# Reordering the first attention of a diffusion backbone, moving conditioning-vector work to the norms, and placing tiles at multiples of 256 bytes

## The chip, the cores and the metric

The kernel runs on one core of one Trainium2 chip, in one launch. Five engines matter: TensorE does matmuls and transposes (PE, with its weight loads as PEld), VectorE is DVE, ScalarE is ACT, GpSimd is POOL, and SyncE (SP) issues nearly all DMAs. Each engine takes its instructions in the order of the program, so an instruction that waits holds up all that stand behind it on its engine. The metric is device microseconds of one execution, lower is better.

## The reference, cut to what matters

256 latent tokens and 256 context tokens, width 1024, two layers. A vector per token kind, SiLU(c) or SiLU(c_ctx), is multiplied by `ada_w` (1024 x 6144 per layer) and gives six conditioning vectors `m[0..5]`: shift, scale and gate ahead of and behind each sub-layer.

```
for l in 0, 1:
    m = split(silu(c) @ ada_w[l] + ada_b[l], 6)         # for latent and for context tokens
    h = rms_norm(x, norm1_g[l]) * (1 + m[1]) + m[0]
    y = even_mixer(h) if l == 0 else odd_mixer(h)       # conv + grouped-query attention; differential attention
    x = x + m[2] * y
    h = rms_norm(x, norm2_g[l]) * (1 + m[4]) + m[3]
    x = x + m[5] * (swiglu(h) if l == 0 else moe(h))    # hidden width 3584; 8 experts, top 2
out = rms_norm(x_latent, final_norm_g)
```

The first attention has 8 query heads of 64 over 2 key heads. Latent queries see 512 keys, context queries 256. Each query and key head is RMS-normed, and latent ones are rotated.

## The kernel before, in words

All is float32. A matrix product is made of three fp32r matmuls (`mm3`, L222 to L225): a value is split into a rounded high part and the rest (`parts`, L233: an ACT copy, then a DVE subtraction). Weights come as blocks of 1 MB. `Stream` holds five landing buffers (`raw0` to `raw4`) and some tiles lent for one load each (`spare`, `once`); `pump` issues the next load on SP as soon as a landing buffer is free, in the order in which the program first uses the blocks. `ws.step()` does the pending DVE part of a split (`low`, L152) and starts the next split (ACT, L140); `ws.get()` forces it.

The order of all engines is the order in which the Python code emits (a manual schedule). The stages, with their places in the profiled span: first norm, convolution and projections up to about 160 us; the first attention (160 to 249); its output projection (to 298); the norm of the dense SwiGLU and the SwiGLU (`ffn_chunk`, 15 steps, to 820); the norm ahead of the second attention and that attention (to about 1030); its output projection, the norm of the experts and the router (to 1061); the experts (to the end).

Conditioning vectors. `ada_half` (L329) makes half of one vector in four yields: 16 matmuls of 512 columns that read two `raw` blocks as they are (L339), an ACT copy (L343), four transposes, two small DVE operations. Such halves wait in `fillers`; `fill(n)` runs the next n of these parts wherever it is called. Before the change, `fill` is called in the first attention from iteration 6 on (six halves), in the output projection, in the SwiGLU (six halves), and in the second attention (four).

First attention. `attend(i)` is one iteration of a pipeline over 32 units (a block of 128 queries and a head; context units are 16 to 31). A unit passes `ev_A` (scores, PE, two units at once into two "mm" banks), `ev_max` (DVE), `ev_exp` (ACT), `ev_C` (transposes, PE, into one of two "tr" banks), `ev_parts` (ACT and DVE, reads that bank), `ev_D` (times values, PE, "av" bank), each one iteration later than the one before; `ev_E` finishes four heads. The order inside an iteration is exp, C, A, E, max, parts, D. PSUM has 8 banks: four "mm", two "tr", one "av", one "ad". The query projections sit in `bq = [PS("av"), PS("ad"), PS("mm"), PS("mm")]`, so the last two share the banks that scores use; `q_b(3)` reads the last of them in iteration 2.

Norms. `rms_rows` takes a square with a row sum (ACT, L400), a power (POOL, L390) and a scaling (DVE, L404) for each block of 128 tokens. `norm_into` then transposes, evacuates and splits, and feeds the first matmuls of the stage behind it. Between a stage's last matmul and the first transposes stands `residual` (L947, L948) of the last block and this chain.

Of the kernel before, what the change touches and what calls it, by code (L numbers as in the profile page):

```python
# [195 lines left out]
def build(nc, tc, a, out, order, dbg=None, stop=None):  # L196
# [18 lines left out]
    def SM(n, name="sm", dt=F32):  # L215
        return pool.tile([128, n], dt, name=name, tag=f"sm{n}_{dt}", bufs=12)
# [3 lines left out]
    mm = nc.tensor.matmul  # L220
# [31 lines left out]

    raws = [T([128, 2048], f"raw{i}") for i in range(5)]
# [9 lines left out]
    cst = T([128, 272], "cst")  # L263
# [45 lines left out]
    mhalf = T([128, 16], "mhalf")  # L309
# [10 lines left out]
    lnT = T([128, 8], "lnT")  # L320
# [39 lines left out]
    def run(g, n=10 ** 9):  # L360
        for _ in range(n):
            try:
                next(g)
            except StopIteration:
                return False
        return True

# [173 lines left out]
    ypad = T([128, 4, 2, 286], "ypad", tag="cA")  # L541
# [4 lines left out]
    cw = T([128, 4, 31], "cw")  # L546
# [3 lines left out]
    nc.vector.tensor_copy(cw, p.rearrange("p (j w) -> p j w", j=4)[:, :, 0:31])  # L550
# [4 lines left out]
    diag = T([128, 32], "diag")  # L555
# [139 lines left out]
    def q_proj(t):  # L695
        for k in range(8):
            mm3(bq[t], [x[:, k, t * 128:(t + 1) * 128] for x in hT], [x[:, k % 2, :] for x in un[k // 2]],
                k == 0, k == 7)
# [58 lines left out]
    bq = [PS("av"), PS("ad"), PS("mm"), PS("mm")]  # L757
# [137 lines left out]
    def attend(i):  # L895
        if 2 <= i < n + 2:
            ev_exp(i - 2)
        if 3 <= i < n + 3:
            ev_C(i - 3)
        if i < n and i % 2 == 0:  # L900
            ev_A(i)
        if "E" in last:
            run(last["E"], 1)
        if 1 <= i < n + 1:
            ev_max(i - 1)
        if 4 <= i < n + 4:
            ev_parts(i - 4)
        if 5 <= i < n + 5:
            ev_D(i - 5)
            if i % 4 == 0:  # L910
                last["E"] = ev_E((i - 5) // 8, (i - 5) // 4 % 2)
        if i in (2, 4):
            last["T"] = q_T(2 + i // 4)
        if i in (3, 5):
            last["T"]()
        if i == 2:
            q_b(3)
        ws.step()
        if 8 <= i < 16 and i % 2:
            j = (i - 8) // 2  # L920
            parts(cat[0][:, j, :], cat[1][:, j, :], cs[:, j])
        if i >= 6:
            fill(1)

    for k in range(8):
        mm3(bq[3], [x[:, k, 384:512] for x in hT], [x[:, k % 2, :] for x in un[k // 2]], k == 0, k == 7)
        if k % 2:
            ws.done(("win", 2, k // 4), k // 2 % 2)
        if 2 <= k <= 5:
            ln_cols(k - 2)  # L930
        if k == 5:
            attend(0)
# [24 lines left out]
    fillers += [ada_half(0, 5, 0)]  # L957
# [13 lines left out]
    for i, kk in enumerate((0, 1, 2, 3)):  # L971
        un = w_out_w(0, kk)
        for t in range(4):
            w_out(0, kk, t, bo[t], un, i == 0, i == 3)
        ws.done(("wout", 0, 0, kk // 2), kk % 2)
        ws.step()
        if i >= 1:
            run(gg, 2)
        fill(2)
    for t in range(4):  # L980
        residual(t, 0, 512, bo[t], g)
    fill(10 ** 6)
    uns = {kk: w_out_w(1, kk) for kk in (0, 1, 2, 3)}
    fillers += [ada_half(0, 5, 1)]
    for t in range(4):
        bank = PS("mm")
        for i, kk in enumerate((0, 1, 2, 3)):
            w_out(1, kk, t, bank, uns[kk], i == 0, i == 3)
            if t == 3:
                ws.done(("wout", 0, 1, kk // 2), kk % 2)  # L990
                ws.step()
        residual(t, 512, 1024, bank, g, nc.vector)
        run(rr, 1)
    run(rr)
# [9 lines left out]
    fill(10 ** 6)  # L1004
    h2 = new_h("h2")
    first = [PS("mm") for _ in range(2)]
    un0 = [[t.rearrange("p (k n) -> p k n", k=4) for t in ws.get(("fg", 0), h)] for h in range(2)]
# [8 lines left out]
    fillers += [ada(1, m) for m in (1, 0, 2)]  # L1016
# [4 lines left out]
    def ffn_chunk(c):  # L1021
# [29 lines left out]
        if c >= 1:  # L1051
            hl = hid.pop(c - 1)
            un = [ws.get(("fd", c - 1), h) for h in range(2)]
            i = 0
            for t in range(4):
                for o in range(2):
                    p = PS(("tr", "tr", "av")[i % 3])
                    for f in range(2):
                        mm3(p, [x[:, f, t * 128:(t + 1) * 128] for x in hl],
                            [x[:, o * 512:(o + 1) * 512] for x in un[f]], f == 0, f == 1)  # L1060
                    residual(t, o * 512, o * 512 + 512, p, g, nc.vector if c == 14 else None)
                    i += 1
                    if i in (2, 4):
                        ws.step()
                    if i == 6 or i == 3 and c % 3 == 0:
                        fill(1)
                if c == 14:
                    run(rr, 1)
            ws.done(("fd", c - 1), 0, 1)
            ws.step(2)  # L1070
# [8 lines left out]
    fill(10 ** 6)  # L1079
    for t in range(4):  # L1080
        dump(f"x2_{t}", X[t])
# [7 lines left out]
    fillers += [ada(1, m) for m in (4, 3)]  # L1089
    fill(2)  # L1090
# [256 lines left out]

    while plan:
# [31 lines left out]
    w_done(1, 3)  # L1380
    for t in range(2):
        residual(t, 512, 1024, bo[1, t], g, nc.vector)
        run(rr, 1)
    for t in range(2):
        dump(f"x3_{t}", X[t])
# [11 lines left out]
    run(a15[0], 1)  # L1397
# [8 lines left out]
    run(a15[1], 1)  # L1406
# [502 lines left out]
```

## Time and profile before

| | us |
|---|---|
| median of 3 runs | 2080.54 |
| lowest and highest run | 2078.64, 2083.23 |
| the profiled execution's own time | 2079.71 |
| its span from first to last instruction | 2077.9 |

The span is the profiled execution; its own time is 1.8 us longer, for what lies around it. PE is busy 96% of the span, DVE 71%, ACT 55%, POOL 12%. A busy PE is not always a PE at full speed: the profile also gives the clock that TensorE was granted in a stretch (1.00 is 2.4 GHz, 0.50 is 1.2 GHz).

### The profile page before, as it was taken

To read this page: it belongs to the slowest core of one execution; us is meant where nothing else is said; L and a number is where in the kernel's file an instruction comes from. 1 tells how busy PE (TensorE), PEld (TensorE's weight loads), DVE (VectorE), ACT (ScalarE), POOL (GpSimd) and SP (SyncE) were. 2 spreads that over 40 slices of the span, in tenths; PEclk is the share of its full clock that TensorE was granted. 3 is DMA by queue.
4 is the path that set the end of the run, shared out by engine and by line. 5 is a ranking of instruction groups with operands and counts; after the bars stand their busy time and mean duration, and the time that the engine had idled before them with its cause. 6 is when DMAs were issued, how large, how long until landed. Compare 5 with 4: busy or idle time off the path is not lost.

```text
span 2077.9 us, 28499 instructions
## 1 busy us (share of the span) xinstructions
PE 1995.2 (96%) x10806; PEld 1606.3 (77%) x10806; DVE 1476.7 (71%) x1918; ACT 1147.5 (55%) x1576; POOL 245.1 (12%) x222
## 2 busy tenths in 40 slices
PE   6998899999999998999989999999999999999987
PEld 4866677777777776989868888888888888888876
DVE  3535443545545456666568999998989999999997
ACT  3215433222222223434457878778787878878765
POOL 0310010323324243011110000000000000000020
PEclk9999899999999999999889999999999999999999
DMA  8303632334333223332488999999999999999972
GB/s 313 124 21 122 231 135 84 139 121 141 132 113 101 81 102 116 119 139 98 143 328 293 353 361 346 358 364 365 356 350 353 372 362 352 346 358 370 351 302 90
DMA packets 98639, 483.39 MB, mean 233 GB/s; under 512 B 12170, under 2 KB 12834, under 8 KB 51649
## 3 DMA queue, kind: packets, MB, share of 16 engines
q1 hardware_dynamic: 96128, 479.84, 63.0%
q8 instruction: 86, 1.41, 0.3%
q10 hardware_dynamic: 2368, 1.68, 0.3%
q14 instruction: 57, 0.46, 0.1%
HBM read 480.43 MB, written 1.05 MB: 232 GB/s over the span
## 4 chain that ended last, share of the span: by engine, by line
PE 57%; DVE 2%; ACT 1%; issue 0%; DVEq 0%; POOL 0%; ACTq 0%; POOLq 0%
PE mm L223 12%; PE mm L224 12%; PE mm L225 12%; PE av L225 3%; PE av L224 3%; PE av L223 3%; PE ad L223 2%; PE ad L224 2%; PE ad L225 2%; PE tr L313 2%; DVE wlo L152 1%; PE tr L1592 1%; PE tr L1518 1%; PE tr L1470 0%; PE ad L339 0%
## 5 line engine op out<-in xcount | busy, mean ns | idle before, releaser
L140 ACT CAST whi<-raw 128x1024 fp32r<-128x1024 f32 x420 | 434.8, 1049 | 248.7 <-PE tr L225 102.8
L152 DVE TENSOR_TENSOR wlo<-raw,whi 128x1024 fp32r<-128x1024 f32 x420 | 550.7, 1346 | 11.9 <-ACT whi L140 8.4
L224 PE MATMUL mm<-wlo,xghi 128*128 128x512 f32 x896 | 351.8, 393 | 5.1 <-DVE wlo L152 5.0
L223 PE MATMUL mm<-whi,xghi 128*128 128x512 f32 x896 | 355.4, 397 | 0.0
L225 PE MATMUL mm<-whi,xglo 128*128 128x512 f32 x896 | 351.0, 392 | 0.0
L948 POOL TENSOR_TENSOR x<-x,tmp 128x512 f32<-128x512 f32 x110 | 163.4, 1516 | 468.1 <-DVE tmp L947 467.8
L140 ACT CAST whi<-spare 128x512 fp32r<-128x512 f32 (+1 forms) x282 | 188.9, 708 | 46.8 <-PE mm L225 27.7
L152 DVE TENSOR_TENSOR wlo<-spare,whi 128x512 fp32r<-128x512 f32 (+1 forms) x282 | 212.5, 794 | 0.0
L224 PEld LDWEIGHTS mm<-wlo,xghi 128*128 128x128 f32 x896 | 168.9, 189 | 43.2 <-DVE wlo L152 8.2
L225 PEld LDWEIGHTS mm<-whi,xglo 128*128 128x128 f32 x896 | 168.8, 188 | 37.1
L223 PEld LDWEIGHTS mm<-whi,xghi 128*128 128x128 f32 x896 | 168.9, 189 | 35.4
L223 PE MATMUL mm<-h2hi,whi 128*128 128x512 f32 x448 | 179.4, 401 | 0.9 <-ACT h2hi L234 0.9
L224 PE MATMUL mm<-h2lo,whi 128*128 128x512 f32 x448 | 178.2, 398 | 0.3 <-DVE h2lo L235 0.2
L225 PE MATMUL mm<-h2hi,wlo 128*128 128x512 f32 x448 | 177.6, 396 | 0.0
L1044 DVE TENSOR_TENSOR silu<-mm,silu 128x512 f32<-128x512 f32 x28 | 19.4, 692 | 191.5 <-PE mm L225 191.5
L152 DVE TENSOR_TENSOR wlo<-rawx,whi 128x1024 fp32r<-128x1024 f32 x112 | 135.1, 1221 | 5.0 <-ACT whi L140 1.6
L140 ACT CAST whi<-rawx 128x1024 fp32r<-128x1024 f32 x112 | 117.4, 1052 | 31.9 <-PE mm L225 27.6
L1605 POOL MEMSET fgain<- 128x1 f32 x1 | 0.1, 98 | 906.9 <-DVE wlo L152 906.9
L223 PEld LDWEIGHTS mm<-h2hi,whi 128*128 128x128 f32 x448 | 84.7, 189 | 24.2 <-issue 3.4
L224 PEld LDWEIGHTS mm<-h2lo,whi 128*128 128x128 f32 x448 | 84.7, 189 | 20.8 <-DVE h2lo L235 1.1
L225 PEld LDWEIGHTS mm<-h2hi,wlo 128*128 128x128 f32 x448 | 84.7, 189 | 20.2
L223 PE MATMUL mm<-whi,h3hi 128*128 128x256 f32 x320 | 93.7, 293 | 1.3 <-ACT h3hi L234 1.3
(395 smaller groups left out, 3849.4 us busy)
## 6 DMA issues: line engine op xcount, KB each, us to landing
raw<-in_t_g_dram SPq DMA_DIRECT2D x81, 1024.0 KB, 7.4
rawx<-in_t_u_dram SPq DMA_DIRECT2D x53, 1024.0 KB, 6.9
raw<-in_t_ada_dram SPq DMA_DIRECT2D x38, 1024.0 KB, 4.9
raw<-in_t_u_dram SPq DMA_DIRECT2D x30, 1024.0 KB, 7.5
raw<-in_t_d_dram SPq DMA_DIRECT2D x30, 1024.0 KB, 7.2
spare<-in_t_g_dram SPq DMA_DIRECT2D x56, 512.0 KB, 7.0
spare<-in_t_u_dram SPq DMA_DIRECT2D x112, 256.0 KB, 6.8
rawb<-in_t_d_dram SPq DMA_DIRECT2D x27, 1024.0 KB, 7.2
```

The lines of the kernel that those rows point to most:

```text
L140: self.nc.scalar.copy(hi[:, i * n:(i + 1) * n], x)
L152: self.nc.vector.tensor_tensor(lo[:, c], x, hi[:, c].bitcast(F32), op=OP.subtract)
L223: mm(o, L[0], R[0], start=first, stop=False)
L224: mm(o, L[0], R[1], start=False, stop=False)
L225: mm(o, L[1], R[0], start=False, stop=last)
L313: nc.tensor.transpose(o, i, ident[:i.shape[0], :i.shape[0]])
L948: (eng or nc.gpsimd).tensor_tensor(X[t][:, c0:c1], X[t][:, c0:c1], tmp, op=OP.add)
L1044: nc.vector.tensor_tensor(sg[j], p, sg[j], op=OP.mult)
L1518: mm(p[:, i * 256:i * 256 + 256], x[:, t, k * 128:k * 128 + 128], S[:, t].rearrange("p j n -> p (j n)"), start=n == 0 and t == 0, stop=n = ...
L1592: mm(p, PT[:, t * 128:(t + 1) * 128], hl[q][:, o * 512:(o + 1) * 512], start=q == 0, stop=q == 1)
L1605: nc.gpsimd.memset(fgain[0][:, 0:1], 0.0)
```

## The change

Four things. (1) In `attend` the order becomes E, D, parts, A, exp, C, max; fillers run from iteration 3, two parts in each of iterations 3 to 6 and one from 7. (2) The query projections alternate between the "av" and "ad" banks, so that the four "mm" banks hold scores alone. (3) Halves of conditioning vectors move: a new function `between` emits the first matmuls of two halves, then the rest of the norm's row chain, then the other parts; three halves stand there at the SwiGLU's norm, and two at the second attention's norm with one more in the SwiGLU's last step. They come out of the output projection (two) and of the SwiGLU's loop (three) and of the second attention (one). `ada(1, 3)` moves later within the second attention, and both halves of `(1, 5)` send their matmuls ahead of the expert norm's transposes. Some `ws.step()` calls near the norms go or move behind the residuals. (4) Small tiles are merged, padded or given more buffers (`misc`, `cst`, `ypad`, `cw`, `SM`), so that large tiles start at multiples of 256 bytes.

```diff
-        return pool.tile([128, n], dt, name=name, tag=f"sm{n}_{dt}", bufs=12)
+        return pool.tile([128, n], dt, name=name, tag=f"sm{n}_{dt}", bufs={1: 16, 8: 18}.get(n, 12))
...
+    misc = T([128, 32], "misc")
+    mhalf, lnT = misc[:, 0:16], misc[:, 16:24]
     raws = [T([128, 2048], f"raw{i}") for i in range(5)]
...
-    cst = T([128, 272], "cst")
+    cst = T([128, 320], "cst")
+    diag, cst = cst[:, 288:320], cst[:, 0:272]
...
+    def between(halves, mid):
+
+        gs = [ada_half(*x, ("ad", "av")[i % 2], "tr") for i, x in enumerate(halves)]
+        for g in gs[:2]:
+            run(g, 1)
+        mid()
+        for g in gs[:2]:
+            run(g, 1)
+        for g in gs[2:]:
+            run(g, 1)
+        for g in gs:
+            run(g)
...
-    ypad = T([128, 4, 2, 286], "ypad", tag="cA")
+    ypad = T([128, 4, 2, 288], "ypad", tag="cA")[..., 0:286]
...
     def q_proj(t):
+        bq[t] = PS(("av", "ad")[t % 2])
...
-    bq = [PS("av"), PS("ad"), PS("mm"), PS("mm")]
+    bq = {}
...
     def attend(i):
+        if "E" in last:
+            run(last["E"], 1)
+        if 5 <= i < n + 5:
+            ev_D(i - 5)
+        if 4 <= i < n + 4:
+            ev_parts(i - 4)
+        if i < n and i % 2 == 0:
+            ev_A(i)
         if 2 <= i < n + 2:
             ev_exp(i - 2)
         if 3 <= i < n + 3:
             ev_C(i - 3)
-        if i < n and i % 2 == 0:
-            ev_A(i)
-        if "E" in last:
-            run(last["E"], 1)
         if 1 <= i < n + 1:
             ev_max(i - 1)
-        if 4 <= i < n + 4:
-            ev_parts(i - 4)
-        if 5 <= i < n + 5:
-            ev_D(i - 5)
-            if i % 4 == 0:
-                last["E"] = ev_E((i - 5) // 8, (i - 5) // 4 % 2)
+        if 5 <= i < n + 5 and i % 4 == 0:
+            last["E"] = ev_E((i - 5) // 8, (i - 5) // 4 % 2)
...
-        if i >= 6:
-            fill(1)
-
+        if i >= 3:
+            fill(2 if i < 7 else 1)
+
+    bq[3] = PS("ad")
...
-    fillers += [ada_half(0, 5, 0)]
...
-        fill(2)
     for t in range(4):
         residual(t, 0, 512, bo[t], g)
-    fill(10 ** 6)
     uns = {kk: w_out_w(1, kk) for kk in (0, 1, 2, 3)}
-    fillers += [ada_half(0, 5, 1)]
...
                 ws.done(("wout", 0, 1, kk // 2), kk % 2)
-                ws.step()
         residual(t, 512, 1024, bank, g, nc.vector)
         run(rr, 1)
-    run(rr)
+    un0 = [[t.rearrange("p (k n) -> p k n", k=4) for t in ws.get(("fg", 0), h)] for h in range(2)]
+    between(((0, 5, 0), (0, 5, 1), (1, 1, 0)), lambda: run(rr))
...
-    fillers += [ada(1, m) for m in (1, 0, 2)]
+    fillers += [ada_half(1, 1, 1), ada(1, 0)]
...
-                    if i in (2, 4):
+                    if i in (2, 4) and c < 14:
                         ws.step()
...
                 if c == 14:
                     run(rr, 1)
+                    if t == 0:
+                        fill(10 ** 6)
+                        fillers.append(ada_half(1, 2, 0))
+                    fill(1)
...
     fill(10 ** 6)
+    between(((1, 2, 1), (1, 4, 0)), lambda: run(rr))
...
-    fillers += [ada(1, m) for m in (4, 3)]
-    fill(2)
+    fillers += [ada_half(1, 4, 1)]
...
+    fillers += [ada(1, 3)]
     while plan:
         beat()
         fill(1)
...
-    w_done(1, 3)
     for t in range(2):
         residual(t, 512, 1024, bo[1, t], g, nc.vector)
         run(rr, 1)
+    w_done(1, 3)
...
     a15 = [ada_half(1, 5, i, "mm", "tr") for i in range(2)]
-    run(a15[0], 1)
+    for x in a15:
+        run(x, 1)
...
     run(a15[0], 1)
-    run(a15[1], 1)
```

## Rows read from the trace of the kernel before

**Rows 1.** Spans view: span and granted clock of the core.
```profile
core 0: 2077.9 us, clock 0.980
```
**Rows 2.** Windows view, three stretches of the first attention: busy us (x instructions), clock, DMA.
```profile
160.90:174.30 13.40, 8.23 (x33) 5.69 (x33) 8.08 (x15) 6.93 (x17) 1.64 (x1) 0.62 0.00 1
174.30:222.00 47.70, 45.54 (x371) 32.14 (x370) 29.12 (x67) 29.25 (x76) 0.00 (x0) 1.00 0.50 186
222.00:249.40 27.40, 21.84 (x129) 16.54 (x129) 18.12 (x45) 14.35 (x42) 0.00 (x0) 0.75 0.75 269
```
**Rows 3.** Windows view, half-clock stretches: first attention (two), the two norms.
```profile
164.10:174.30 10.20, 8.20 (x32) 5.69 (x33) 5.74 (x11) 4.00 (x12) 0.00 (x0) 0.50 0.01 2
239.20:249.40 10.20, 8.20 (x31) 7.03 (x32) 4.97 (x13) 3.78 (x10) 0.00 (x0) 0.50 0.78 248
304.10:314.30 10.20, 8.69 (x26) 6.54 (x26) 7.05 (x13) 4.51 (x8) 0.00 (x0) 0.50 0.69 265
822.90:833.10 10.20, 7.03 (x29) 6.04 (x29) 6.86 (x11) 5.56 (x11) 2.26 (x3) 0.50 0.61 225
```
**Rows 4.** Source view of L872, 222 to 246 us: duration ns min/median/max.
```profile
L872 PE MATMUL av<-v,pt x52: 272/306/472, 221.8 to 244.5; 128*128 128x128 f32 x52
```
**Rows 5.** Waits of PE, 150 to 250 us: us in total, times, longest.
```profile
PE tr L313 <- DVE pt L235: 5.2, 9, 1.1
PE mm L231 <- DVE qn L659: 3.7, 1, 3.7
```
**Rows 6.** Timeline, start of the first attention: start, us, instruction, idle before it.
```profile
163.37 0.68 ACT L822 ACTIVATE p<-mm,nm 128x512 f32<-128x512 f32 x1
163.81 0.69 DVE L659 TENSOR_TENSOR qn<-mm,r 128x512 f32<-128x512 f32 x1 [0.56 <-POOL r L390]
```
**Rows 7.** Windows view, from the last output-projection matmul to the SwiGLU's first.
```profile
298.20:307.80 9.60, 5.21 (x34) 2.98 (x33) 7.77 (x15) 5.36 (x10) 1.97 (x2) 0.80 0.83 321
```
**Rows 8.** Timeline at that norm: a filler's matmuls, the loads it lets go.
```profile
298.29 1.92 PE L339 MATMUL ad<-raw,s 128*32 128x512 f32 x16
298.97 0.81 SPq L94 DMA_DIRECT2D raw<-in_t_ada_dram  x2
```
**Rows 9.** DMA issues of conditioning blocks: KB each, median us to landing.
```profile
raw<-in_t_ada_dram SPq DMA_DIRECT2D x38, 1024.0 KB, 4.9
```
**Rows 10.** Timeline of that norm's chain, last block: residual, square, scaling; then the first matmul.
```profile
299.99 0.68 DVE L947 TENSOR_TENSOR tmp<-mm,gate 128x512 f32<-128x512 f32 x1
...
301.49 1.06 ACT L400 ACTIVATE xnB<-x 128x1024 f32<-128x1024 f32 x1 [2.10 <-issue]
...
303.92 0.75 DVE L404 TENSOR_SCALAR xnB<-x,r 128x1024 f32<-128x1024 f32 x1 [0.44 <-POOL r L390]
...
307.77 0.80 PE L223 MATMUL mm<-h2hi,whi 128*128 128x512 f32 x1 [0.86 <-ACT h2hi L234]
```
**Rows 11.** Windows view, from the SwiGLU's last matmul to the second attention's first.
```profile
818.10:828.80 10.70, 5.18 (x29) 2.66 (x28) 9.41 (x18) 6.41 (x10) 4.13 (x4) 0.72 0.60 207
```
**Rows 12.** Waits of PE, 795 to 840 us.
```profile
PE av L223 <- DVE tmp L947: 2.4, 2, 1.2
```
**Rows 13.** Timeline there: the splits on DVE and ACT beside the residuals.
```profile
810.76 2.35 DVE L152 TENSOR_TENSOR wlo<-raw,whi 128x1024 fp32r<-128x1024 f32 x2
823.02 1.98 ACT L140 CAST whi<-raw 128x1024 fp32r<-128x1024 f32 x2
```
**Rows 14.** Waits of PE, 1040 to 1075 us (the experts' norm).
```profile
PE mm L313 <- DVE xnA L404: 3.3, 2, 2.4
```
**Rows 15.** Windows view, the transposes of that norm.
```profile
1048.20:1051.60 3.40, 3.40 (x18) 2.70 (x16) 1.96 (x4) 2.41 (x5) 0.00 (x0) 0.50 0.90 302
```
**Rows 16.** Waits of PE, 0 to 60 us.
```profile
PE mm L223 <- ACT whi L140: 2.8, 1, 2.8
```
**Rows 17.** Windows view, one stretch of the expert stage.
```profile
1650.00:1675.00 25.00, 25.00 (x115) 20.54 (x114) 22.50 (x25) 20.05 (x25) 0.00 (x0) 1.00 1.00 382
```

## What the prediction says, on record before the run

> **What bounds the kernel now.** I read the spans first: the core's mean TensorE clock is 0.980 over 2077.9 us [rows 1], so 2 x 0.020 x 2077.9 = 83 us run at half speed, 1.2 GHz. The page says PE is busy 96% of the span, and in the expert stage, the second half of it, each stretch shows PE busy throughout at full clock [rows 17]. Nothing in the diff touches that stage's work, so the question is what the first 1070 us hold besides full-speed matmuls. Two things can be taken out there: PE idle, and PE at half clock. The windows show both in four places: the first attention [rows 2, 3], the SwiGLU's norm [rows 3, 7], the second attention's norm [rows 3, 11], the experts' norm [rows 14, 15]. The price of half clock is read from one line that ran at both: a values matmul takes 272 ns at its shortest and 472 at its longest [rows 4], so of each busy us at half clock 1 - 272/472 = 0.42 is lost.
>
> What each place holds over full-speed work: the attention's start has 13.4 - 8.2 = 5.2 idle and 8.20 x 0.42 = 3.5 lost, 8.7 us; its middle 2.2 idle; its tail 27.4 - 21.8 = 5.6 idle and, at clock 0.75, 13.7 us of half clock, of which 10.2 hold 8.2 busy and the other 3.5 I take as all busy, 11.7 x 0.42 = 4.9 lost, so 10.5 [rows 2, 3]. The SwiGLU's norm has 9.6 - 5.2 = 4.4 idle and 8.69 x 0.42 = 3.7 lost, 8.1 [rows 3, 7]. The second attention's norm has 10.7 - 5.2 = 5.5 idle, 7.03 x 0.42 = 3.0 lost, and one wait of 1.2 in the SwiGLU's last step, 9.7 [rows 3, 11, 12]. The experts' norm has 3.3 idle and 3.4 x 0.42 = 1.4 lost, 4.7 [rows 14, 15]. A moved half brings its matmuls along, so moving costs nothing on PE and gains only what it covers of these 43.9 us.
>
> **Attention, start.** The second pair of scores gets one bank at 160.43 and waits 3.7 us for the other, which query projection 3 holds until the DVE has read it at 163.81 [rows 5, 6]. With projections in "av" and "ad", both banks are free, and the pair can run at once. What is late next is the first transpose: it needs the first exp, which ends where the second begins, at 163.37 [rows 6], 2.0 us after a pair that ends near 161.4 (six matmuls); behind it, the first filler needs "ad", free at 163.81 + 0.69 = 164.5, about 0.5 later. The fillers now start in iteration 3, which gives PE two halves (2 x (1.92 + 0.6) = 5 us, the matmuls by [rows 8], four transposes estimated at 0.15 each) in iterations 3 to 6. I leave 1.9 us idle, once the transposes of queries take their place in it, and 1.0 for what else waits. If no half clock follows, 8.7 becomes 2.9: gain 5.7. Bounds: 1.5 (half clock as now) and 8.7.
>
> **Attention, middle.** Nine waits of transposes for the low part of an earlier unit cost 5.2 us [rows 5]: C stands first on PE in an iteration and needs the bank that parts, last on DVE, has just read. Parts first turns that round; the middle holds 2.2 of idle in all [rows 2]. The new order adds a wait: `ev_E`'s transposes take a fifth bank of scores in every fourth iteration, while A of the same iteration needs two and exp, which frees one, now stands behind A in the code and behind parts on ACT. On PE, C, the fill and max's input queue behind A. D and E's two transposes cover most of it; I keep 0.2 in each of four, and take 0.7 left, gain 1.5. Bounds: -1 and 2.2.
>
> **Attention, tail.** Seven filler parts that ran in iterations 23 to 29 are gone from there, so PE has less to do between waits. The tail already shows half clock where waits fall between 128-column matmuls. Half clock from iteration 23 on is the bound: its work without fillers is 21.8 - 4.9 - 4.4 (seven quarters of a 2.5 us half) = 12.5 at full speed, and at half speed it costs 12.5 x 0.73 = 9.1 with 5 idle beside it, 14 against 10.5; the best is 8. I take 11.7, loss 1.2. The Trainium skill, in "TensorE: Matmul & The Clock Gate", A second HAM failure mode: psum-queue depth-cycling, tells of a kernel whose short pauses between groups of matmuls, as it cycles PSUM banks, kept dropping its clock; the clock of 0.75 here agrees. By that rule alone the tail would go to its bound, 14, 2.3 us worse than my value.
>
> Attention together: 5.7 + 1.5 - 1.2 = 6.0, bounds -3 and 13.
>
> **SwiGLU's norm.** From the end of the output projection, T, the last residual now goes first on DVE (before, it started at 299.99 behind splits [rows 10], 1.5 us late). But `un0` forces two casts and two DVE splits of 1.2 us (half of the pair in [rows 13]) between the square and the last power, so the scaled rows are ready near T + 6.4 - 1.5 + 2.4 + 1.0 (one cast, half of a pair in [rows 13]) = T + 8.3 instead of T + 6.4. Two halves' matmuls cover T to T + 3.8. The third half is the trouble: five landing buffers hold one SwiGLU block and the four blocks of (0, 5), so its two loads can be issued only as these are used, the first 0.7 us after the matmuls begin [rows 8], and land 4.9 later [rows 9], with the second some 2.5 behind, at T + 8. Its 1.92 us, its copy and twelve transposes follow, the norm's transposes come near T + 10.5, and the first dense matmul, 3 us on as now (304.67 to 307.77 [rows 10]), at T + 13.3. Useful work in that: 3 x 1.92 + 1.8 + 1.3 = 8.9, so 4.4 idle; I add 0.9 for clock and steps. 8.1 becomes 5.3: gain 2.8. Bounds: -1.7 (half clock as well) and 6.
>
> **Second attention's norm.** In the SwiGLU's last step the DVE loses a 2.35 us pair of splits between residuals [rows 13], which removes the wait of 1.2 there, and one half runs beside it. From its end, U, two halves cover U to U + 3.8; the rows are ready at U + 5.2 (1.5 residual, 3.2 the chain from square to scaling as in [rows 10], 0.5 for the removed overlap with the residual before it). The removed splits now stand ahead of `norm_into`: DVE gets four of 1.2 us where two stood, the first evacuation on DVE comes near U + 10.3 and the first matmul at U + 11.6, against 10.7 now. With 3.8 + 1.2 + 1.3 useful, 5.3 stay idle, and about 1.7 of clock and wait: 9.7 becomes 6.7 (the wait in the last step left at 0 or so), gain 3.0. Bounds: -0.5 and 7.
>
> **Experts' norm.** Both halves of (1, 5) go ahead of the transposes, so 1.9 us more of the 3.3 is covered and the half clock in [rows 15] may go. But both now hold an "mm" bank, leaving two of four for eight transposed blocks, and the rows still end near 1047.5, since POOL and DVE, not the moved step, set them. Gain 0.7. Bounds: -1.5 and 3.
>
> **256 bytes.** No instruction changes, only where tiles lie: every SBUF address of a load. What could follow is at the start, where one wait of 2.8 for freshly cast weights hangs on loads [rows 16]. I take 0.7; bounds 0 and 2.8. Smaller: `ada(1, 3)` moves inside a stretch that PE fills either way, 0 (bounds 1 each way, a wait of the 3.3 kind that it could meet being bounded by its matmuls' 1.92).
>
> **Sum.** 6.0 + 2.8 + 3.0 + 0.7 + 0.7 = 13.2. The profiled execution took 2079.7 (2077.9 and 1.8 around it), so 2066.5; the median of the runs shown stands 0.8 above it: **2067 us**.
>
> **The rivals.**
> *The clock stays up at the norms too.* For it: PE's longest idle at both norms becomes shorter. Against: 128-column transposes stay there. Attention 9, norms 5 and 6, experts' 2, start 1.5: 23.5 less, 2057.
> *Waits only change places.* The third half's loads hold PE, ACT stands in casts of late blocks, the tail falls to half clock: attention 3.5, norms 0 and 0, the rest 0.5: 2077. For it: five buffers, and 4.9 us per load [rows 9].
> *Slower: half clock spreads.* One mechanism, TensorE's clock: pauses are cut up but stay, among small matmuls, and the half-speed time grows. 10.2 us more of it with 8.2 busy costs 3.5 [rows 3]. The gains in idle come to about 9; from some 26 us more of half-speed time it decides, and with 45 more (the tail, both norms, and the transposes behind the router) the time is 2080.5 - 9 + 15.5 = 2087. Against it: matmuls of 512 columns, which stand here at full clock for whole stages, are what is moved in.
> *Transfers were the bound.* If the expert stage, with its DMA share of 1.00 [rows 17], ran at the transfers' pace, faster packets would shorten some 950 us of it: each 1% is 9.5 us. Against: PE is busy throughout there and waits for none. The Trainium skill, in "DMA: Bandwidth & Descriptors", How a descriptor splits into AXI transactions, says a transfer that doesn't start at a multiple of 256 bytes takes one more transaction than an aligned one; an estimate from that page is 1 in 33 for 8 KB, 3%, and with it this rival gives some 2040. No run here has yet shown an aligned transfer.
>
> **How the numbers follow.** A difference of 0.2%, 4.2 us, is about what runs of one kernel scatter (2078.64 to 2083.23) and what can be told from no change. Forecast 0.49 (own range 2060 to 2073); clock up everywhere 0.19; waits change places 0.20; slower 0.09; transfers 0.03. Faster is the first two, the last, and a quarter of the third that ends under 2076.4: 0.76. Same is the rest of the third, 0.15; slower 0.09. The range leaves out the slower case, the transfers and the ends of the others: 2053 to 2080.
>
> **What would show it.** Right: scores of the second pair right behind the first with no 3.7 us wait, few waits of transposes for low parts, a clock near 1.00 through iterations 6 to 22; fewer us at half speed than 83; PE waiting for the third half's blocks at the SwiGLU's norm; four splits on DVE ahead of the second norm's evacuation. Wrong: half clock from iteration 23 through the output projection, or at both norms as long as now; any wait of PE in the expert stage; a span under 2050.

## The result and the profile after

The changed kernel takes 2058.32 us (median of 4 runs, 2055.73 to 2062.08) where the kernel before, run beside it, took 2080.14: ratio 0.9895, interval 0.9873 to 0.9916, so 21.8 us less. Forecast were 2067 and a range of 2053 to 2080. The range holds it, but the gain is 1.6 times the forecast, and most of it comes from a part that the sum priced at 0.7. The profiled execution of the changed kernel is the slowest of its four, 2062.08.

The spans view first, which answers to [rows 1]:

```profile
core 0: 2060.2 us, clock 0.979
```

The span is 17.7 us shorter, and the mean clock is not higher: 2 x 0.021 x 2060.2 = 87 us at half clock, where there were 83. So in this execution the gain is not a gain in clock, and the rival "the clock stays up", nearest to the result by its number (2057), is not what happened in it. The three other runs had mean clocks of 0.982 to 0.987, which is 53 to 74 us at half clock, so the median gain holds a few us of clock besides.

The windows view of the changed kernel (start:end us, length, busy us and instructions of PE, PEld, DVE, ACT, POOL, granted clock, DMA share, GB/s), in this order: the half-clock stretch of the attention's tail, that at the SwiGLU's norm, that at the experts' norm; then the whole of the SwiGLU's norm, the second attention's norm, the attention's start and the rest of the attention.

```profile
218.50:245.80 27.30, 25.41 (x114) 22.21 (x113) 13.77 (x37) 11.82 (x40) 0.00 (x0) 0.50 0.32 114
297.00:307.30 10.30, 5.35 (x24) 1.98 (x25) 1.42 (x4) 0.59 (x1) 0.71 (x1) 0.50 0.95 372
...
1034.30:1058.20 23.90, 20.52 (x84) 19.32 (x84) 7.89 (x28) 9.28 (x17) 4.87 (x4) 0.50 0.84 344
290.60:311.20 20.60, 11.01 (x73) 4.59 (x73) 8.22 (x19) 7.16 (x12) 1.98 (x2) 0.75 0.67 268
806.40:818.90 12.50, 6.12 (x54) 3.01 (x53) 10.15 (x20) 7.60 (x12) 3.15 (x3) 1.00 0.85 334
159.30:170.60 11.30, 8.94 (x62) 5.02 (x61) 6.08 (x11) 7.27 (x15) 1.64 (x1) 1.00 0.23 76
170.60:240.80 70.20, 66.84 (x477) 52.13 (x475) 47.72 (x112) 43.28 (x118) 0.00 (x0) 0.84 0.56 207
```

Against [rows 2, 3] the start of the attention is at full clock, and its tail has one half-clock stretch of 27.3 us instead of two that come to 13.6. The SwiGLU's norm, 9.6 in [rows 7], is 20.6 long, half of it idle.

PE's waits from 150 to 250 us (us in total, times, longest), beside [rows 5]:

```profile
PE tr L317 <- ACT p L838: 1.5, 1, 1.5
...
PE tr L317 <- DVE pt L235: 0.8, 2, 0.4
```

The wait of 3.7 for `qn` is gone, and the nine waits of 5.2 for the low parts are two of 0.8: those two steps went as forecast. The 1.5 is the wait for the first exp, left at 1.9 in the forecast.

Where the rest went is seen by cutting every run at the same instructions. The table is worked out from start and end times of PE's matmuls in the traces, in us. "start" is from the first scores to the first values matmul, "rest" from there to the output projection; the norms run from the last matmul of the stage before to the first dense one behind; "att2" includes its output projection.

```
kernel            start rest  oproj norm1 SwiGLU norm2 att2  to experts  experts  median
before            16.1  72.6  51.7   9.4  510.4  10.6  213.6   24.9      996.5   2080.5
e1_align_only     14.6  71.0  51.4   9.5  501.2  10.6  215.2   27.5      992.0   2066.5
e2_no_align       12.2  66.2  49.8  20.3  503.3  12.5  206.4   26.9      996.3   2072.5
after             11.3  70.2  49.8  20.6  495.3  12.5  207.4   26.8      993.0   2058.3
e3_shift96        12.7  64.5  47.4  20.1  495.3  12.5  208.4   25.8      992.5   2054.7
e4_hf_align       11.3  64.6  49.0  20.4  495.2  12.5  207.3   26.9      984.5   2047.4
e5_attend_only    12.2  70.7  51.8   9.4  509.0  10.6  213.0   25.8      995.8   2074.3
e6_two_halves     11.3  70.4  49.5  13.1  498.3  12.5  207.7   25.3      983.9   2045.3
e7_tail_fill      11.3  68.2  49.0  21.5  495.9  12.5  207.8   25.4      984.0   2050.5
e8_ada13_early    12.6  70.1  48.8  20.2  495.3  15.5  212.2   25.8      984.2   2058.6
e9_un0_late       12.7  64.6  47.5   9.7  499.2  12.5  208.3   25.4      984.2   2037.9
e10_steps_back    12.3  69.5  49.4  13.0  505.2  10.6  208.4   25.8      984.2   2045.4
e11_norm1_old     12.3  70.9  51.2   9.5  498.2  12.5  207.7   25.4      984.1   2046.5
e12_steps_apart   11.3  64.6  49.1   8.9  481.4  12.5  208.0   25.4      984.0   2021.8
```

One half of a conditioning vector costs PE about 2.5 (1.92 of matmuls and four transposes), and which stage holds it is to be kept in mind: from "oproj" to "SwiGLU" the kernel before and e1, e5 have eight halves, all others seven, and those have one more in "norm2" and "att2".

Two things stand out. The SwiGLU and the experts, 15.1 and 3.5 shorter between before and after, are stages where the change moves two halves at most. And with the same halves in them, in before against e1 and in e2 against after, both stages are shorter where part (4) is in.

### The profile page after: what moved, and what is told of

Its sections match the earlier page's. It is cut to its first block, busy times and chain, and to the rows that moved or that the text cites. A ratio compares the mean times of both kernels' runs of the same rounds, so it can differ in the third digit from the quotient of the medians.

```text
span 2060.2 us, 28489 instructions
## 1 busy us (share of the span) xinstructions
PE 1976.6 (96%) x10806; PEld 1607.9 (78%) x10806; DVE 1475.3 (72%) x1918; ACT 1148.9 (56%) x1576; POOL 246.0 (12%) x222
## 4 chain that ended last, share of the span: by engine, by line
PE 90%; DVE 4%; ACT 2%; issue 1%; DMA 1%; POOL 0%; ACTq 0%; DVEq 0%; SPq 0%; POOLq 0%
PE mm L223 18%; PE mm L224 18%; PE mm L225 18%; PE av L223 4%; PE av L225 4%; PE av L224 4%; PE tr L317 3%; PE ad L223 3%; PE ad L225 3%; PE ad L224 3%; PE tr L223 2%; PE tr L225 2%; PE tr L224 2%; PE mm L596 2%; DVE wlo L152 1%
## 5 line engine op out<-in xcount | busy, mean ns | idle before, releaser
L152 DVE TENSOR_TENSOR wlo<-raw,whi 128x1024 fp32r<-128x1024 f32 x414 | 544.0, 1350 | 23.8 <-ACT whi L140 19.2
L140 ACT CAST whi<-raw 128x1024 fp32r<-128x1024 f32 x414 | 429.6, 1051 | 232.1 <-PE tr L225 100.0
L140 ACT CAST whi<-spare 128x512 fp32r<-128x512 f32 (+1 forms) x282 | 188.7, 707 | 43.9 <-PE mm L225 24.9
L152 DVE TENSOR_TENSOR wlo<-rawx,whi 128x1024 fp32r<-128x1024 f32 x118 | 143.4, 1239 | 4.8 <-ACT whi L140 1.5
L140 ACT CAST whi<-rawx 128x1024 fp32r<-128x1024 f32 x118 | 124.2, 1055 | 38.7 <-PE mm L225 35.0
```

Of the source, the lines that this page charges most:

```text
L140: self.nc.scalar.copy(hi[:, i * n:(i + 1) * n], x)
L152: self.nc.vector.tensor_tensor(lo[:, c], x, hi[:, c].bitcast(F32), op=OP.subtract)
```

## The experiments

### Where tiles lie: e1 to e4

e1_align_only is the kernel before with part (4) alone, the diff of the tiles shown above. e2_no_align is the changed kernel with that part undone. e3 and e4 change the changed kernel in one line each:

```diff
# e3_shift96
-    misc = T([128, 32], "misc")
+    misc = T([128, 56], "misc")
# e4_hf_align
-bufs={1: 16, 8: 18}.get(n, 12))
+bufs={1: 16, 8: 18, 6: 11}.get(n, 12))
```

> The kernel before with part (4) of the change alone: small tiles merged and padded so that large tiles start at multiples of 256 bytes; every instruction and its order stay. Theory A, alignment paid most of what the prediction missed: 512-column matmuls start about 227 ns apart in the SwiGLU where they stood 233 apart, which over its 1344 matmuls with h2 and some 3400 others is 10 to 12 us: 2068 to 2071. Theory B, the prediction's own sum (alignment 0.7): 2079 to 2080. If the transfers were the bound: 2065 or less, with shorter packets.

> The changed kernel without part (4): tiles lie where they lay before, the orders of the attention, of the halves and of the splits stay changed. Theory A: the matmuls of the SwiGLU are 233 ns apart again, 10 to 12 us lost: 2068 to 2071. Theory B: 2058 to 2060, since 12.5 us or more come from the orders.

> The changed kernel with 96 bytes added to the first tile, so that every later tile moves by 96 bytes and none starts at a multiple of 256, while the distances between tiles stay. Theory A1, what counts is whether the moving and the stationary operand of a matmul start at the same place modulo 256: nothing changes, 2057 to 2060, 227 ns in the SwiGLU. Theory A2, multiples of 256 count in themselves: 2068 to 2071, 231 to 234 ns.

> The changed kernel with one small buffer of 32 bytes fewer ahead of the last large tile, so that hF, the stationary operand of the experts' second product, moves from 32 to 0 modulo 256 (it is the one large tile that the change left off). Theory A: its 1344 matmuls go from 233 to 227 ns, 8.3 us less: 2049 to 2051. Rival: the expert stage then goes at the pace of its transfers (a share of 0.9 to 1.0) or of the DVE's splits, and PE waits instead: 2056 to 2059.

Measured: e1 2066.5, ratio 0.9942 (0.9924 to 0.9960), 12.1 us less than before (8 to 16), with every instruction in its old place. e2 2072.5, ratio 0.9962 (0.9947 to 0.9976), 14 above the changed kernel. e3 2054.7, ratio 0.9887 (0.9869 to 0.9904): no loss. e4 2047.4, ratio 0.9840 (0.9824 to 0.9857), 10.9 below the changed kernel by median, 8.5 in the experts' stage.

The windows view over the SwiGLU, of the kernel before and then of e1, shows the same work in 9.2 us less, with PE as busy and the clock as high:

```profile
307.80:818.20 510.40, 494.91 (x2192) 389.29 (x2196) 263.13 (x282) 127.48 (x165) 154.33 (x105) 0.99 0.32 112
```

```profile
302.60:803.80 501.20, 485.03 (x2191) 388.06 (x2191) 263.73 (x282) 127.73 (x165) 154.26 (x105) 1.00 0.32 114
```

What is shorter is the distance from one matmul to the next. The timeline of PE, 96 matmuls of the SwiGLU's first product without a wait between them, first and last: of the kernel before,

```profile
666.52 0.39 PE L223 MATMUL mm<-h2hi,whi 128*128 128x512 f32 x1
...
688.62 0.40 PE L225 MATMUL mm<-h2hi,wlo 128*128 128x512 f32 x1
```

and of e3_shift96:

```profile
646.91 0.39 PE L223 MATMUL mm<-h2hi,whi 128*128 128x512 f32 x1
...
668.44 0.39 PE L225 MATMUL mm<-h2hi,wlo 128*128 128x512 f32 x1
```

95 steps take 22.10 before and 21.53 there: 232.6 ns each against 226.6. Over the 1344 matmuls with h2 these 6 ns are 8.1 us of the 9.2 above. The duration of one, 0.39, is the same: it is the time from its start to its modelled end, and the next starts long before that. A reader who compares durations sees nothing; start times must be subtracted. In the first case h2, the operand that moves through the array, starts at 96 and most of the split weights, the stationary operand, at 160 modulo 256 bytes; in e3 both start at 96. So a multiple of 256 is not what counts; the two operands of a matmul starting at the same place modulo 256 is. That 256 is the modulus is also seen within one trace: in e4 the operands of 512-column matmuls lie 0, 256, 512 or 768 bytes apart modulo 1024, and all four groups have a median of 227 ns. e4 shows it on one tile: `hF`, which the change left at 32 while the weights went to 0. The timeline of 24 matmuls of the experts' second product, after and then e4:

```profile
1310.18 0.39 PE L223 MATMUL av<-whi,hF 128*128 128x512 f32 x1
...
1315.54 0.40 PE L225 MATMUL ad<-whi,hF 128*128 128x512 f32 x1
```

```profile
1303.09 0.39 PE L223 MATMUL av<-whi,hF 128*128 128x512 f32 x1
...
1308.31 0.39 PE L225 MATMUL ad<-whi,hF 128*128 128x512 f32 x1
```

23 steps in 5.36, 233 ns, and in 5.22, 227 ns. Over 1344 matmuls that is 8.2, and the stage is 8.5 shorter. The rival, that transfers or DVE would take over the pace, fell: the stage is shorter by what its matmuls gained.

### The attention alone: e5

Its diff is that of `attend`, `bq` and `q_proj` shown above, and the line `fill(2 if i < 7 else 1)` from iteration 3.

> The kernel before with parts (1) and (2) alone: the new order in the attention, its fillers from iteration 3, and the query projections in the banks av and ad. The prediction's term: 6.0 less, 2074 (bounds 2067 and 2083): start of the attention 4 to 6 shorter with six filler parts in it, the stretch behind it about level for that work. Rival, the stages of the runs so far are read rightly: from the first scores to the output projection 88.7 becomes 78 to 80 with the clock up in the tail, 82 with it down: 2070 to 2074. Other rival, the attention gained through its neighbours alone: 2079 to 2080.

Measured: 2074.3, ratio 0.9978 (0.9967 to 0.9989): 4.6 less (2.3 to 6.9), and this interval holds the predicted 6.0. From the first scores to the output projection 88.7 became 82.9. The timeline of PE at the end of the start, in e5:

```profile
167.09 2.81 PE L339 MATMUL ad<-raw,s 128*32 128x512 f32 x16 [0.38 <-DVE qn L659]
...
172.34 0.60 PE L313 MATMUL ad<-ident,row 128*128 128x128 f32 x4
172.69 1.09 PE L873 MATMUL av<-v,pt 128*128 128x128 f32 x8
```

The start is 3.9 shorter with four filler parts more in it, one half, 2.5 us of PE at full clock: the matmuls at 167.09 and the transposes at 172.34, ahead of the first values matmul. The expectation counted six, but in iteration 5 `ev_D` stands ahead of the fillers. So the start gained 6.4. The rest is 1.9 shorter with four parts fewer, so it lost 0.6: here the tail is at half clock from 222.6 to 246.5.

That tail is not settled by the order of instructions. The windows view of "rest" in e4 and in e6, two kernels that have the same instructions up to there:

```profile
171.90:236.50 64.60, 59.98 (x477) 44.72 (x475) 47.66 (x112) 43.13 (x118) 0.00 (x0) 1.00 0.62 226
```

```profile
168.90:239.30 70.40, 67.04 (x478) 52.46 (x475) 47.71 (x112) 43.26 (x118) 0.00 (x0) 0.84 0.57 207
```

One execution kept 2.4 GHz, the other fell to 1.2 GHz at 216.4, and that is 5.8 us. The table has both kinds among kernels with the same instructions there: 64.5 or 64.6 in e3, e4, e9 and e12, 69.5 to 70.9 in after, e6, e8, e10 and e11, and 66.2 in e2, where half clock began at 230.7. So a difference of some 6 us between two medians below must be checked against the stages before it is put down to an edit.

### Fillers in the tail: e7

```diff
-        if i >= 3:
+        if 3 <= i < 7 or i >= 14:
             fill(2 if i < 7 else 1)
```

> The kernel of e4_hf_align with the attention's filler parts at iterations 3 to 6 (two each) and 14 to 29 (one each) instead of 3 to 22, so that parts lie between the tail's waits again. Theory of the prediction's tail term: without parts the tail runs at half clock in some runs; with them the stretch from the first values matmul to the output projection is 64 to 66 at full clock in all runs, and the times lie 1 to 4 lower or scatter less: 2043 to 2047. Rival: the middle, now without parts, waits more and falls to half clock in turn: 2047 to 2052.

Measured: 2050.5, ratio 0.9860 (0.9837 to 0.9882), 3 above e4. Its profiled execution was at half clock from 227.4 to 241.1 all the same, for 13.7 us. So parts between the tail's waits did not keep the clock up in it, and the rival has the number; but its mechanism, half clock in the middle, was not seen.

### The SwiGLU's norm: e6, e9, e11

Here is the largest miss of the other sign. In the changed kernel PE has one wait of 7.4 there. The timeline around it (start, us, instruction, idle before):

```profile
290.50 1.92 PE L342 MATMUL ad<-raw,s 128*32 128x512 f32 x16
...
294.22 2.36 DVE L152 TENSOR_TENSOR wlo<-raw,whi 128x1024 fp32r<-128x1024 f32 x2 [1.47 <-ACT whi L140]
...
296.61 0.80 SPq L94 DMA_DIRECT2D raw<-in_t_ada_dram  x2
...
301.52 1.93 PE L342 MATMUL ad<-raw,s 128*32 128x512 f32 x8 [7.38 <-DMA raw<-in_t_ada_dram]
...
311.16 0.49 PE L223 MATMUL mm<-h2hi,whi 128*128 128x512 f32 x1 [1.78 <-ACT h2hi L234]
```

The first half's matmuls, from 290.50, let buffers go, and the prediction had the third half's loads issued 0.7 behind their start, at 291.2. They were issued at 296.61, 0.03 after the DVE split that `un0` forces ended (294.22 + 2.36 = 296.58). The first buffer that SP's queue waits for, in program order, is that of the split. The load into it, here the first block of the third half itself, stands first in SP's queue and holds up the rest. Landing then took 4.9, as in [rows 9].

```diff
# e6_two_halves, against e4 (two lines that only set up the vector are left out)
-    between(((0, 5, 0), (0, 5, 1), (1, 1, 0)), lambda: run(rr))
+    between(((0, 5, 0), (0, 5, 1)), lambda: run(rr))
-    fillers += [ada_half(1, 1, 1), ada(1, 0)]
+    fillers += [ada(1, 1), ada(1, 0)]
# e9_un0_late, against e6: the same line, moved from ahead of between to behind norm_cols
-    un0 = [[t.rearrange(...) for t in ws.get(("fg", 0), h)] for h in range(2)]
     between(((0, 5, 0), (0, 5, 1)), lambda: run(rr))
...
     first = [PS("mm") for _ in range(2)]
+    un0 = [[t.rearrange(...) for t in ws.get(("fg", 0), h)] for h in range(2)]
# e11_norm1_old, against e6: oproj and norm1 as in the kernel before
+    fillers += [ada_half(0, 5, 0)]
...
+        fill(2)
...
+    fillers += [ada_half(0, 5, 1)]
...
+                ws.step()
...
-    between(((0, 5, 0), (0, 5, 1)), lambda: run(rr))
+    run(rr)
...
# un0 is asked for behind norm_cols, as in e9
```

> The kernel of e4_hf_align with two halves instead of three at the SwiGLU's norm; the third, (1, 1, 0), goes back into the SwiGLU's loop. Theory: its loads hold PE there (one wait of 7.4 in the changed kernel); from the last output-projection matmul to the SwiGLU's first 20.4 becomes 12 to 14, the loop takes 2.4 more: 4 to 6 less than e4, 2041 to 2043.5. Rival: the row chain behind two forced splits holds PE as long, and the stage is 17 to 18: 2047.

> The kernel of e6_two_halves with the first SwiGLU splits asked for behind the norm's coefficients, as in the kernel before, instead of ahead of the row chain. The prediction's step: forced ahead, they put two casts and two DVE splits into the chain and make its rows 1.9 late; so the stage at the norm goes from 13.1 to 11 or less: 2042.5 to 2044, against e6 at 2045.3. Rival: the splits are then what the first dense matmul waits for, and nothing is gained or 1 to 3 are lost: 2045 to 2048.

> The kernel of e6_two_halves with the output projection and the SwiGLU's norm as in the kernel before: the two halves (0, 5, 0) and (0, 5, 1) in the output projection, splits among its residuals, no halves between the square and the power; the rest as in e6. The prediction's term, worked for two halves: moving them to the norm gains 3 to 4, so this is 2048 to 2050. Rival, halves there only take the place of other waits: output projection, norm and SwiGLU together stay at 561 within 1, 2044.5 to 2046.5.

Measured: e6 2045.3, ratio 0.9831 (0.9808 to 0.9854); e9 2037.9, 0.9799 (0.9782 to 0.9815); e11 2046.5, 0.9840 (0.9826 to 0.9855). By stages, which leave the attention's clock out: output projection, norm and SwiGLU, with the same seven halves in each, are 564.6 in e4, 560.9 in e6, 556.4 in e9 and 558.9 in e11. So the third half cost 3.7 (4 to 6 were expected). The splits asked for late shorten the norm by 3.4, of which 0.9 comes back in the SwiGLU; the output projection's 2.0 between e6 and e9 is half clock that reaches into it in e6. So the edit of e9 is worth 2.5. The prediction's step has 2.4 + 1.0 = 3.4 for the forced splits, which is what the norm alone shows; the 1.9 of the expectation takes off the 1.5 of the earlier residual, which e9 keeps. The two profiled executions are 9.6 apart, and the 7.8 in "rest" and "oproj" are the clock's; so the medians, 7.4 apart, overstate the edit, and e9's 2037.9 lies below both of its forecasts. The order of the kernel before, e11, is 5.7 better than the change's in e4. Two halves at the norm are 1.4 to 2.5 better than the order before, which has the matmuls of one of them there already [rows 8], once neither fault is there (the lower end if the half clock in the first 2.7 us of e11's output projection is taken off at 0.42), less than the 3 to 4 expected.

SP's queue and the split in e6, where it is forced ahead, and in e9, where it is not:

```profile
288.73 1.92 PE L342 MATMUL ad<-raw,s 128*32 128x512 f32 x16
...
292.45 2.36 DVE L152 TENSOR_TENSOR wlo<-raw,whi 128x1024 fp32r<-128x1024 f32 x2 [1.48 <-ACT whi L140]
...
294.84 0.33 SPq L94 DMA_DIRECT2D raw<-in_t_fu_dram  x1
```

```profile
281.48 1.92 PE L342 MATMUL ad<-raw,s 128*32 128x512 f32 x16
282.61 0.33 SPq L94 DMA_DIRECT2D raw<-in_t_fu_dram  x1
```

The first load goes out 6.1 after the half begins in e6 (294.84 is 0.03 behind the split's end, 294.81), 1.1 after it in e9.

### The second attention: e8 and e10

```diff
# e8_ada13_early, against e4
-    fillers += [ada_half(1, 4, 1)]
+    fillers += [ada_half(1, 4, 1), ada(1, 3)]
+    fill(2)
...
-    fillers += [ada(1, 3)]
     while plan:
# e10_steps_back, against e6
-                    if i in (2, 4) and c < 14:
+                    if i in (2, 4):
```

> The kernel of e4_hf_align with ada(1, 3) put back where it stood before, ahead of the second attention's projections, with two of its parts run there at once. The prediction's term: 0, 2047 (within 2). Rival: without parts in the last iterations of the second attention TensorE falls to half clock there, as the kernel before shows (13.6 us at 0.50), 4 to 6 lost: 2051 to 2053.

> The kernel of e6_two_halves with the splits back between the residuals of the SwiGLU's last step. The prediction's step: without them DVE has four splits ahead of the second norm's evacuation; back in place, the wait of 1.2 in the last step returns and the wait of 4.8 for the first h3hi becomes about 2.4: between 1.5 less and 0.5 more than e6, 2043.5 to 2046. Rival: POOL and the row chain set the rows' time, and only the wait of 1.2 comes back: 2046 to 2047.

Measured: e8 2058.6, ratio 0.9895 (0.9866 to 0.9924), 11 above e4; in the profiled executions the first attention's tail makes 5.5 of the difference (64.6 against 70.1 in "rest"), which the edit does not touch. From the SwiGLU's end to the experts 246.7 became 253.5, 6.8 more: 3.0 at the norm, where `fill(2)` sends a half first, and the rest at the end of the second attention. The windows view there, of e8 and of e4:

```profile
989.80:1003.50 13.70, 13.12 (x51) 10.04 (x51) 11.50 (x27) 7.32 (x17) 3.41 (x9) 0.50 0.50 158
```

```profile
981.00:994.70 13.70, 12.42 (x88) 8.81 (x87) 11.75 (x30) 7.27 (x17) 3.28 (x8) 1.00 0.96 372
```

The half-clock stretch of the kernel before returned with the early `ada(1, 3)`. The move is worth 4 to 7 and was priced at 0.

e10 took 2045.4, ratio 0.9832 (0.9817 to 0.9846), level with e6: of the splits taken out between the residuals no effect on the time can be told. Its norm is 1.9 shorter and the wait for the first h3hi 3.6 instead of 4.8, but the SwiGLU before it is 6.9 longer in the profiled execution, which at 2052.04 is the slowest of the five. The timeline there shows why:

```profile
798.25 1.04 ACT L140 CAST whi<-raw 128x1024 fp32r<-128x1024 f32 x1 [6.14 <-DMA raw<-in_t_odin_dram]
...
800.87 1.12 PE L317 MATMUL ad<-ident,row 128*128 128x128 f32 x4 [4.68 <-ACT row L346]
```

A cast that the edit put back waited 6.14 for its block and held up, on ACT, the copy of a filler's row; PE waited 4.68 for that copy (0.5 in e6), and the clock was at half from 799.9 to 806.7. So in this execution the splits cost more in the SwiGLU than they gain at the norm, as a block landed late; by the medians nothing can be told.

### Waits that the change left: e12

```diff
# against e9
-                    ws.step(1 + j)
+                    ws.step(1 + j if kind == "fg" else 1)
...
-                    if i in (2, 4) and c < 14:
+                    if i in (2, 6) and c < 14:
```

> The kernel of e9_un0_late, and in each step of the SwiGLU one split fewer is started at the end of its second product, with the second of the two splits among the residuals moved from behind the fourth to behind the sixth. This is no part of the change: it goes for the 12 waits of 1.25 that stand in all kernels so far, where a residual in the av bank stands on DVE behind two splits (3.96 in e9). Theory: PE sets the pace of the SwiGLU and the waits fall away, 12 x 1.25 = 15 less: 2023 (2021 to 2027). Rival: the split that is left out is missing at the next step's first matmul, and the waits move there: 2034 to 2042.

Measured: 2021.8, ratio 0.9720 (0.9703 to 0.9737), 16.1 below e9. PE's waits for residuals in the SwiGLU, in e9 and then in e12:

```profile
PE av L223 <- DVE tmp L964: 15.1, 12, 1.3
```

```profile
PE tr L223 <- DVE tmp L964: 1.0, 1, 1.0
```

Twelve waits of 1.25 went and one of 1.0 came. The stage is 17.8 shorter, more than the 14 that this makes, because such a wait costs more than its idle time. One of them, in e9:

```profile
633.44 0.39 PE L225 MATMUL tr<-whi,hidlo 128*128 128x512 f32 x1
635.08 0.50 PE L223 MATMUL av<-whi,hidhi 128*128 128x512 f32 x1 [1.25 <-DVE tmp L964]
635.41 0.40 PE L224 MATMUL av<-wlo,hidhi 128*128 128x512 f32 x1
```

From start to start these are 1.64 and 0.33 where two steps at 0.227 take 0.45, so 1.52 is lost; twelve times that is 18. e12 is the fastest version here, 58 us below the kernel before.

## Why the prediction was right, and where it was not

It was right in sign and range. The sum of 13.2 was made of terms that missed on both sides and partly cancelled.

**256 bytes** is the step that failed, in the sentence "No instruction changes, only where tiles lie ... I take 0.7; bounds 0 and 2.8". The bound came from one wait at the start; e1 measured 12.1. The prediction had set aside the stages where PE is busy throughout at full clock [rows 17] and taken that as a floor. It was none: PE busy at 1.00 says nothing of the distance between matmuls, and the trace of before held medians of 233 and of 227 ns side by side, for `mm<-h2hi,whi` and `tr<-whi,hidhi`, which have one shape. What the runs showed in its place: a 512-column matmul whose operands start at different places modulo 256 takes longer to the next, by some 6 ns for h2 and hF.

**Transfers as the bound** did not come to pass. Page part 3, the queue that carries nearly all, before and in e1 (packets, MB, share of 16 engines' span):

```profile
q1 hardware_dynamic: 96128, 479.84, 63.0%
```

```profile
q1 hardware_dynamic: 96128, 479.84, 63.3%
```

0.630 x 2077.9 = 1309 and 0.633 x 2063.5 = 1306: the packets took as long with every landing tile of the weights at 0 modulo 256 in SBUF (e1) as with `raw` at 128 and the lent ones at 32 to 224 (before), and the 8 KB ones have a median of 309 ns in both traces. By the Trainium skill, "DMA: Bandwidth & Descriptors", How a descriptor splits into AXI transactions, a transfer that starts off a multiple of 256 bytes takes one transaction more, and an estimate of 3% from it was weighed; the trace doesn't agree for the SBUF side, where these loads are written and which is all that this change moves.

**The other rivals.** Of "waits only change places" one part came true: the third half's loads held PE, for 7.4. "Half clock spreads" did not, with 87 us against 83 in the profiled executions.

**Attention**: 6.0 predicted, 4.6 measured (2.3 to 6.9). The start gained 6.4 in e5 (3.9, and 2.5 of parts taken in) and 7.3 in the changed kernel (4.8 and 2.5), more than 5.7: of its 10.2 us at half clock 3.4 were left in e5, from 168.0, and none in the changed kernel. The tail falls to half clock for 10 to 27 us in some executions and keeps full clock in others; the value of 11.7, between the ends, described neither. In the changed kernel's profiled execution it was at half clock from 218.5 into the output projection, which the prediction had named as a sign of being wrong. By the Trainium skill, "TensorE: Matmul & The Clock Gate", A second HAM failure mode: psum-queue depth-cycling, short idle times between groups of matmuls keep the clock going up and down, and by that the tail would go to its bound; the trace of e5 agrees (23.9 us at 0.50), that of e4 doesn't ("rest" at 1.00).

**SwiGLU's norm**: gain 2.8 predicted, with bounds of -1.7 and 6; a loss of 5.7 by stages (e4 against e11). "The first 0.7 us after the matmuls begin" failed: SP's queue was blocked by the load behind the forced split, 5.4 later. First dense matmul at T + 20.6, not T + 13.3 (T = 290.57). That the forced splits delay the row chain was right, and e9 shows its size: 3.4 at the norm, 2.5 in all.

**Second attention's norm**: the first dense matmul came at U + 12.5; U + 11.6 was predicted. The stage of 10.6 before was not without a half: the sixteen matmuls of one stand at its start.

```profile
818.11 1.92 PE L339 MATMUL ad<-raw,s 128*32 128x512 f32 x16
```

It became 12.5 with two whole halves, which is 3.1 more of work (1.92, and 1.14 for eight transposes): 1.2 gained there. The wait of 1.2 in the SwiGLU's last step went too, which makes 2.4 where 3.0 was forecast (and the sum's own 5.3 and 1.7 make 7.0 and not 6.7, a gain of 2.7). That is read from stages, no run isolates it, and e10 found nothing for the splits by the medians.

**Experts' norm**: 0.7 predicted. 24.9 to 27.5 in the old order, 25.3 to 26.9 in the new: none can be told. The half clock at its transposes [rows 15] did not go: the changed kernel has 23.9 us of it from 1034.3.

**`ada(1, 3)`**, "moves inside a stretch that PE fills either way, 0": wrong by 4 to 7, since what it fills is the stretch in which the clock fell. The windows view of the kernel before shows that stretch, which the prediction's four places leave out:

```profile
1000.40:1014.00 13.60, 13.15 (x52) 10.07 (x52) 11.45 (x27) 7.30 (x17) 3.31 (x9) 0.50 0.50 161
```

At the prediction's own price, 13.15 x 0.42 = 5.5 could be had there.

Added up: 12.1 for the tiles, 4.6 for the attention, and for part (3) the distance from e5 to e2, where 6.5 was forecast for the three norms: 1.8 by medians, 3.3 by their ratios to the kernel before, run beside each (0.9978 and 0.9962). In pieces that is 5.7 lost at the SwiGLU's norm, 2.4 gained at the second attention's, and 4 to 7 gained by `ada(1, 3)`. The sum is 18.5 to 20.0; each term carries 2 to 4 us, so the 21.8 measured is met within that. Rows of the trace bear out the mechanisms of alignment (e1, e3, e4), of the blocked queue (e9) and of `ada(1, 3)` (e8). What decides the attention's tail clock from one execution to the next stays open.

## What to carry to other kernels

An engine that is busy throughout at full clock can still run 2.5% slow (6 of 233 ns here): compare the start-to-start distance of matmuls of one shape between tile groups before calling a stage saturated. Give the moving and the stationary tile of a 512-column product the same offset modulo 256 bytes; the size or count of one small tile ahead of them is enough. When loads are moved, ask what stands ahead of them in the issuing queue, not only when their buffer comes free; and judge small edits by stages, since clock in an unrelated stage can move a median by 6 us.

## What the hardware showed that was not expected

Start-to-start distance at full clock (medians, or the lowest and highest median of the groups), worked out from the traces, with the offsets of moving and stationary operand modulo 256 from the compiled programs:

```
columns  offsets moving, stationary    ns          seen in
512      160,160 / 96,96 / 0,0         226 to 227  before, e3, after
512      96,160                        233 to 234  before, h2 with weights
512      160,0 / 0,32 / 96,128         232 to 235  before, after, e3: hF
512      160,192                       230 to 235  before
512      160,32 and 160,96             226 to 232  before
256      160,96                        118         before, h3
256      0,0                           120         after, h3
```

At 256 columns the sign is the other way: equal offsets cost 2 ns more, some 2 us over 960 matmuls, and "att2" of e1 is 1.6 longer than before. Why either is so was not tested. That the same instructions end the attention at either clock from one execution to another (64.6 or 70.4) was the other surprise.
